# A streaming-encoder block on one core: four low parts per dense group by an adding transfer, and pair 13 by seven products

## The chip, the cores and the metric

The kernel runs on one core of one Trainium2 chip. The metric is the time on the device in microseconds (us), from the first to the last instruction of one execution of the program. Three runs of the kernel before the change took 2028.84 to 2030.45 us, with a median of 2029.99 us.

The engines have short names here: PE does matrix products (PEld is its weight load, which overlaps them), DVE is the vector engine, ACT the scalar engine, POOL is GpSimd, and SP issues most of the transfers. POOL can issue transfers too, and a transfer that POOL issues may add to what lies in its destination.

## What is computed

One layer of a hybrid encoder on x of shape (1, 256, 4096), all in float32:

```python
xn = rms_norm(x, norm_in_g)
q, k, v, z_a, a_c, g_c, z_c = split(xn @ w_in)             # w_in: 4096 x 14336
y_a = chunked_attention(q, k, v, rel_table)                # 2048 columns
y_a = rms_norm(y_a, attn_out_g) * silu(z_a)
y_c = conv_module(a_c, g_c, w_dw, ..., w_pw, b_pw)         # 2048 columns
y_c = rms_norm(y_c, conv_out_g) * silu(z_c)
h = x + concatenate([y_a, y_c]) @ w_out                    # 4096 x 4096
gate = sigmoid(rms_norm(h, ple_norm_g) @ w_ple_gate + b)   # 4096 x 4096
h = h + gate * (p @ w_ple)
out = rms_norm(h, final_g)
```

Three products with weights of 4096 rows carry nearly all of the work. The weights are read from HBM once.

## The kernel before

**Parts.** A float32 product is done as three products of shorter numbers. Each operand is split into a high part (a copy rounded to a shorter format, `fp32r`) and a low part (the number minus its high part). PE computes high x high, low activation x high weight, and high activation x low weight. The activations are split once and kept: `xT` (the input), `yT` (attention and convolution) and `hT` (the residual) are eight tiles each of four blocks, with the high and low part of 128 rows of k by 256 tokens per block. The weights are split as they stream by (`parts_of`, L199): ACT casts the tile `wt` to `wh` (L204) and DVE subtracts, `wl = wt - wh` (L205). A `wt` tile holds 128 rows of k for two column blocks of 512, 512 KB; SP issues its transfer. Five buffers hold `wt`, three each hold `wh` and `wl`.

**Products.** `mixed_product` (L344) computes two column blocks j for two halves h of the tokens, with four PSUM banks `acc`. Its k blocks are taken in 16 pairs, in an order given by a text such as `dense` (L329). A pair without a mark is plain: two tiles, 24 matmuls. A pair with "*" goes by seven products instead of eight, in the manner of Strassen: 21 matmuls. For it DVE also forms sums of weights, `ua` (L469, L470) and `ub` (L476, L477), which are split like weights into `uh` and `ul`, and four products read activation blocks that were combined beforehand (`s_of`, out of `comb` tiles). Four helper banks (`acc_P` in the profile) hold the extra products until `on_helpers` adds them up after the last seven of the group. A pair with "+" (early groups only) has its `ua` summed by a transfer of POOL that adds to what SP loaded (L423).

**Groups.** A group is one call of `mixed_product`. `dense` orders nine of them: the four groups for z of `gated` (L1064; 986 to 1314 us of the profile), the last three of w_out (1404 to 1651 us) and the last two of `gated_pair` for w_ple_gate (1743 to 1918 us). The first groups of w_out and w_ple_gate, in which their operands are still being made, use `late`, and the last group of all uses `final`. In all dense groups pairs 1, 3, 5, 7, 9, 11, 13 and 15 are plain.

At the end of a group, four evacuations read the `acc` banks: DVE adds them to the sums of the helpers (L1051 for the last product of the convolution, L1075 in `gated`, L1201 in `gated_pair`). The next group's matmuls cannot write into a bank before. This place is called a seam below. What follows the evacuations (gating, squares, adding to the residual `hc`) is put into a list, `later`, and `fill` takes some of it after each pair; in the profile these side steps have the line L184. In a w_ple_gate group there are twelve of them on DVE besides the four evacuations.

**What sets the order.** A scheduler that knows the dependencies and the tiles' buffers orders the queue of each engine when the program is built; the order of the text is where it starts from. Each engine then works strictly down its queue. An instruction that waits holds up all that stand behind it on its engine.

## Time and profile before

| what | value |
|---|---|
| runs of the kernel, median of 3 | 2029.99 us (2028.84 to 2030.45) |
| profiled execution, its span | 2027.3 us |
| matmuls on PE (`PE ... x`) | 9064 |
| ACT busy | 1222.7 us, 60% |
| `wl` by subtraction, 128x1024 | 601 times, mean 1219 ns from start to end |
| `wh` by cast, 128x1024 | 601 times, mean 1052 ns |
| transfers from HBM | 430.77 MB, 215 GB/s over the span |

The median of the runs and the span of the profiled execution are different measurements. The prediction adds up terms against the span and says how the two stand to each other.

In the timeline a row holds the start, the duration, the engine, the line, the operation, what it writes and reads, its shape and how many of the kind follow one another; in brackets stands how long the engine was idle before it and what ended that. Operations overlap a little at their ends, so that what one costs is better read from start to start. In the windows view each row is a stretch of time; behind each engine stand its busy time and the number of its instructions, then the granted clock of PE, the busy share of the transfer engines and GB/s. The groups' lines (`L205 DVE ...`) give busy time and the mean of one in ns, and behind the second bar the idle time of the engine ahead of them and what ended it.

### The profile page before, as it was taken

What the parts mean: (1) busy time and instruction counts of PE and PEld (TensorE: products, weight loads), DVE (VectorE), ACT (ScalarE), POOL (GpSimd) and SP (SyncE); (2) the same over time, 40 slices, a digit from 0 to 9 for tenths busy, and PEclk for the clock granted to TensorE, in tenths of its full rate; (3) what the DMA queues carried; (4) which work ended last, traced back from release to release, by engine and by line L of the source; (5) the groups of instructions that cost most, each with busy time, mean ns of one, the idle gap of its engine ahead of it and who ended that gap; (6) DMA issues with size and microseconds to landing.
All of it is one profiled execution on the core that took longest, in us unless ns stands there. A gap on an engine that the chain in (4) does not pass through costs nothing.

```text
span 2027.3 us, 26222 instructions
## 1 busy us (share of the span) xinstructions
PE 2010.3 (99%) x9064; PEld 1652.2 (81%) x9064; DVE 1917.8 (95%) x2732; ACT 1222.7 (60%) x1591; POOL 46.9 (2%) x50
## 2 busy tenths in 40 slices
PE   9999999999999999999999999999999999999997
PEld 7888888878888888788888888888888888888876
DVE  7999999889999998888899999999999999999998
ACT  7655545665656556776556566676665666665555
POOL 0000000000000000000000000000000000000000
PEclk9999999999999999999999999999999999999999
DMA  8787878678669867556666666676666656666765
GB/s 293 222 237 236 253 219 249 177 227 256 192 198 268 251 202 239 157 176 213 192 210 204 206 203 214 210 239 209 203 210 199 208 191 204 207 219 205 233 206 181
DMA packets 171168, 436.70 MB, mean 215 GB/s; under 512 B 13966, under 2 KB 17182, under 8 KB 171034
## 3 DMA queue, kind: packets, MB, share of 16 engines
q1 hardware_dynamic: 161952, 417.93, 64.1%
q0 software_dynamic: 8432, 16.25, 4.7%
q8 instruction: 71, 1.16, 0.3%
q10 hardware_dynamic: 650, 0.84, 0.1%
q14 instruction: 63, 0.52, 0.1%
HBM read 430.77 MB, written 4.19 MB: 215 GB/s over the span
## 4 chain that ended last, share of the span: by engine, by line
PE 92%; DVE 4%; issue 2%; DMA 1%; ACT 1%; POOLq 0%; POOL 0%; ACTq 0%; DVEq 0%
PE acc L387 71%; PE acc_P L387 17%; DVE wl L205 1%; PE tmp_ps L170 1%; DVE cv L726 1%; PE acc L229 1%; DMA wt<-in_w_in_dram 1%; DVE ul L205 1%; PE tmp_ps L898 0%; PE tmp_ps L882 0%; PE tmp_ps L916 0%; DVE cv L807 0%; PE tmp_ps L921 0%; ACT uh L204 0%; PE acc L375 0%
## 5 line engine op out<-in xcount | busy, mean ns | idle before, releaser
L387 PE MATMUL acc<-wh,big_t 128*128 128x512 f32 x4112 | 1271.6, 391 | 0.9 <-DVE y_c L1051 0.7
L204 ACT CAST wh<-wt 128x1024 fp32r<-128x1024 f32 (+1 forms) x737 | 708.8, 972 | 514.6 <-PE acc L387 359.8
L387 PEld LDWEIGHTS acc<-wh,big_t 128*128 128x128 f32 x4112 | 768.9, 188 | 160.4 <-DVE y_c L1051 1.1
L205 DVE TENSOR_TENSOR wl<-wt,wh 128x1024 fp32r<-128x1024 f32 (+1 forms) x737 | 816.7, 1120 | 33.4 <-ACT wh L204 27.8
L387 PE MATMUL acc<-wl,big_t 128*128 128x512 f32 x2056 | 794.5, 392 | 0.1
L387 PEld LDWEIGHTS acc<-wl,big_t 128*128 128x128 f32 x2056 | 385.5, 188 | 81.6 <-DVE wl L205 2.0
L204 ACT CAST uh<-ua 128x1024 fp32r<-128x1024 f32 x180 | 189.4, 1052 | 95.9 <-DVE ua L470 46.4
L205 DVE TENSOR_TENSOR ul<-ua,uh 128x1024 fp32r<-128x1024 f32 x180 | 219.5, 1220 | 5.0 <-ACT uh L204 3.2
L726 DVE SCALAR_TENSOR_TENSOR cv<-uT,dw,cv 128x255 f32<-128x255 f32 (+23 forms) x480 | 204.2, 465 | 1.1
L387 PE MATMUL acc_P<-uh,big_t 128*128 128x512 f32 x528 | 161.8, 391 | 0.1
L204 ACT CAST uh<-ub 128x1024 fp32r<-128x1024 f32 x92 | 96.8, 1052 | 92.5 <-DVE ub L477 81.1
L205 DVE TENSOR_TENSOR ul<-ub,uh 128x1024 fp32r<-128x1024 f32 x92 | 112.2, 1220 | 6.3 <-ACT uh L204 5.5
L387 PEld LDWEIGHTS acc_P<-uh,big_t 128*128 128x128 f32 x528 | 98.0, 188 | 23.0 <-ACT uh L204 3.5
L387 PE MATMUL acc_P<-ul,big_t 128*128 128x512 f32 x264 | 101.1, 391 | 0.1
L469 DVE TENSOR_TENSOR ua<-wt 128x512 f32<-128x512 f32 x105 | 72.0, 686 | 17.6 <-DMA wt<-in_w_in_dram 11.5
L387 PE MATMUL acc<-uh,big_t 128*128 128x512 f32 x272 | 84.1, 390 | 0.0
L387 PE MATMUL acc_P<-wh,big_t 128*128 128x512 f32 x272 | 84.0, 389 | 0.0
L470 DVE TENSOR_TENSOR ua<-wt 128x512 f32<-128x512 f32 x105 | 71.8, 684 | 3.2 <-DMA wt<-in_w_in_dram 3.1
L387 PE MATMUL acc_P<-uh,comb_t 128*128 128x512 f32 x228 | 70.2, 391 | 0.4 <-ACT uh L204 0.3
L477 DVE TENSOR_TENSOR ub<-ub,wt 128x512 f32<-128x512 f32 x92 | 63.1, 686 | 0.8
L476 DVE TENSOR_TENSOR ub<-ua,wt 128x512 f32<-128x512 f32 x92 | 62.9, 684 | 0.3
L387 PEld LDWEIGHTS acc<-uh,big_t 128*128 128x128 f32 x272 | 51.1, 188 | 10.6
(244 smaller groups left out, 1518.9 us busy)
## 6 DMA issues: line engine op xcount, KB each, us to landing
wt<-in_w_in_dram SPq DMA_DIRECT2D x416, 512.0 KB, 4.6
wt<-in_w_out_dram SPq DMA_DIRECT2D x128, 512.0 KB, 4.2
wt<-in_w_ple_gate_dram SPq DMA_DIRECT2D x128, 512.0 KB, 4.2
wt<-in_w_pw_dram SPq DMA_DIRECT2D x32, 512.0 KB, 4.7
ua<-in_w_in_dram SPq DMA_DIRECT2D x31, 512.0 KB, 4.5
ua<-in_w_in_dram POOLq DMA_DIRECT2D x31, 512.0 KB, 8.4
wt<-in_w_in_dram SPq DMA_DIRECT2D x31, 256.0 KB, 2.9
hc<-in_x_dram SPq DMA_DIRECT2D x8, 512.0 KB, 4.2
```

The source lines that it names most:

```text
L170: nc.tensor.transpose(pt[:, i * T + h * P : i * T + (h + 1) * P], src[:, h, b] if len(src.shape) == 4 else src[:, h, b * P : (b + 1) * P], ...
L204: nc.scalar.copy(wh[:, :kc, :], wt[:, :kc, :]),
L205: nc.vector.tensor_tensor(wl[:, :kc, :], wt[:, :kc, :], wh[:, :kc, :].bitcast(F32), ALU.subtract),
L229: nc.tensor.matmul(acc, a, b[:, k, :], start=kb == 0 and kind == 0, stop=kb == kblocks - 1 and kind == 2,)
L387: nc.tensor.matmul(banks[name], a, b, start=name not in begun, stop=final and ends[name] == n and kind == 2 and not (left and name in "P2 ...
L469: plus(ua[:, 0], w0[:, 0], w0[:, 1])
L470: plus(ua[:, 1], w0[:, 1], w1[:, 1])
L476: plus(ub[:, 0], ua[:, 0], w1[:, 1])
L477: plus(ub[:, 1], ub[:, 0], w1[:, 0])
L726: nc.vector.scalar_tensor_tensor(cv[:, i, PAD - k :], uT[:, i, : T + k - PAD], dw[:, b, k : k + 1], cv[:, i, PAD - k :], ALU.mult, ALU.add,)
```

## The change

Two things are changed in the nine dense groups, and a new order goes with them.

Four plain pairs (3, 5, 7 and 9) are marked "-". The low part of their second tile is not subtracted by DVE. Instead `high_and_minus` lets ACT make `wh` and, by a second operation, minus the same rounded numbers into a tile `low` (of the tag "stage", two buffers). Then POOL issues a transfer that reads the same weights from HBM once more and adds them onto `low`, which thereby becomes weight minus high part. The four matmuls that read `low` are put off until after the next pair (`waiting`, `add_waiting`). `compare` runs once, in the first dense group: DVE makes that tile's low part by subtraction as well, subtracts `low` from it, ACT squares and sums the difference, and the sum is added to `r_x`.

Pair 13 goes by seven products. Its combined activations have no `comb` tile; they are written into the second half of the tokens' columns of block 0 in four tiles of xT, yT and hT (`spare_places`), three times in all: after the other combinations of xT, after the first w_out group and after the first w_ple_gate group.

The tiles z of `gated` and `gated_pair` are now taken when the helper banks are summed, not at the start of the group.

```diff
+    def high_and_minus(wt):
+
+        wh = wpool.tile([P, KC, NB], F32R, tag="wh", name="wh", bufs=3)
+        nc.scalar.copy(wh, wt)
+        low = spool.tile([P, KC, NB], F32R, tag="stage", name="low")
+        nc.scalar.activation(low, wt, AF.Identity, scale=-1.0)
+        return wh, low
+
+    compared = []
+
+    def compare(wt, wh, low):
+
+        same = wpool.tile([P, KC, NB], F32R, tag="wl", name="wl", bufs=3)
+        nc.vector.tensor_tensor(same, wt, wh.bitcast(F32), ALU.subtract)
+        nc.vector.tensor_tensor(
+            same.bitcast(F32), same.bitcast(F32), low.bitcast(F32), ALU.subtract
+        )
+        apart = cpool.tile([P, KC], F32, name="apart")
+        for k in range(KC):
+            square_sum(apart[:, k : k + 1], same[:, k].bitcast(F32), scale=1e9)
+        nc.vector.tensor_tensor(r_x, r_x, apart, ALU.add)
+        compared.append(True)
...
         def split():
+            if at_places:
+                for i, (hi, lo) in enumerate(at_places):
+                    src = s[:, i * P : (i + 1) * P]
+                    nc.scalar.copy(hi, src)
+                    nc.vector.tensor_tensor(lo, src, hi.bitcast(F32), ALU.subtract)
+                return
...
-    dense = units("1 0* 3 2* 5 4* 6* 7 8* 9 10* 11 12* 14* 13 15")
+    dense = units("1 0* 2* 3- 4* 13* 5- 6* 8* 7- 10* 12* 9- 14* 11 15")
...
+    def spare_places(tiles):
+
+        return [[t[:, 0, q, P:] for q in range(2)] for t in tiles[:4]]
+
+    places = {}
+
+    def combine_into_places(pair, tiles):
+
+        rows = sum_rows()
+        places[pair] = spare_places(tiles)
+        t, i = tiles[pair // 2], pair % 2 * 2
+        combine_again(None, None, t, i, rows, at_places=places[pair])()
...
+        waiting = []
+
+        def add_waiting(n):
+
+            while waiting and waiting[0][0] <= n:
+                waiting.pop(0)[1]()
...
             if not seven:
-                for k in range(2):
-                    add_plain(n, k, *parts_of(wts[k], 2)[0])
+                add_plain(n, 0, *parts_of(wts[0], 2)[0])
+                if by_dma:
+                    wh, low = high_and_minus(wts[1])
+                    nc.gpsimd.dma_start(
+                        low, two_columns(w, 2 * pair + 1, col, apart), accum_op=ALU.add
+                    )
+                    if not compared:
+                        compare(wts[1], wh, low)
+                    add_plain(n, 1, wh, low, kinds=range(2))
+                    waiting.append((n + 1, partial(add_plain, n, 1, wh, low, kinds=(2,))))
+                else:
+                    add_plain(n, 1, *parts_of(wts[1], 2)[0])
+                add_waiting(n)
...
             def s_of(i):
+                if pair in places:
+                    return places[pair][i]
...
             add("P4", block(k1, 1), (ubh[:, 1], ubl[:, 1]), n, True)
+            add_waiting(n)
...
+    combine_into_places(13, xT)
 
     def gated(ys, c0, col, r_y, order, ahead):
 
-        _, z = sum_tiles()
+        z = []
 
         def on_helpers(helper):
+            z.extend(sum_tiles()[1])
...
+        if c0 == 0:
+            combine_into_places(13, yT)
...
     for c0 in range(0, n_f - 2, 2):
         gated_pair(c0, dense if c0 else late, None if c0 else h_ahead)
+        if c0 == 0:
+            combine_into_places(13, hT)
```

The scheduler turns this into other queues. Three places show it. A row holds the line, the operation, what it writes and reads (with the tiles' numbers), and the shape; line numbers behind the change are those of the changed kernel.

The first place is DVE's queue in the first dense group. Before, between pairs 2 and 4 of the order:

```order
L469 TENSOR_TENSOR ua_9055<-wt_9047 128x512
L205 TENSOR_TENSOR ul_8987<-ub_8983,uh_8986 128x1024
L205 TENSOR_TENSOR wl_8980<-wt_8966,wh_8979 128x1024
L470 TENSOR_TENSOR ua_9055<-wt_9047,wt_9049 128x512
L476 TENSOR_TENSOR ub_9066<-ua_9055,wt_9049 128x512
L205 TENSOR_TENSOR wl_9016<-wt_9011,wh_9015 128x1024
L205 TENSOR_TENSOR wl_9032<-wt_9013,wh_9031 128x1024
```

With the change, around the comparison (L225 and L226):

```order
L541 TENSOR_TENSOR ub_8960<-ua_8949,wt_8943 128x512
L205 TENSOR_TENSOR wl_8993<-wt_8988,wh_8992 128x1024
L542 TENSOR_TENSOR ub_8960<-ub_8960,wt_8943 128x512
L225 TENSOR_TENSOR wl_9013<-wt_8990,wh_9008 128x1024
L534 TENSOR_TENSOR ua_9038<-wt_9030 128x512
L205 TENSOR_TENSOR ul_8964<-ub_8960,uh_8963 128x1024
L226 TENSOR_TENSOR wl_9013<-wl_9013,low_9010 128x1024
L205 TENSOR_TENSOR wl_9035<-wt_9030,wh_9034 128x512
L535 TENSOR_TENSOR ua_9038<-wt_9030,wt_9032 128x512
L541 TENSOR_TENSOR ub_9049<-ua_9038,wt_9032 128x512
```

L226 reads `low`, so it stands behind the adding transfer; a `ua` and a `ul` are between it and L225, and the parts of pair 4 are behind it.

The second place is ACT's queue in the third group of `gated`, before:

```order
L204 CAST wh_10352<-wt_10348 128x512
L204 CAST uh_10359<-ua_10356 128x1024
L204 CAST wh_10363<-wt_10350 128x1024
L204 CAST uh_10370<-ub_10367 128x1024
L204 CAST wh_10399<-wt_10395 128x1024
L204 CAST wh_10415<-wt_10397 128x1024
L204 CAST wh_10435<-wt_10431 128x512
```

and with the change:

```order
L204 CAST wh_10368<-wt_10364 128x512
L204 CAST wh_10379<-wt_10366 128x1024
L217 ACTIVATE low_10433<-wt_10413 128x1024
L204 CAST wh_10415<-wt_10411 128x1024
L204 CAST uh_10375<-ua_10372 128x1024
L215 CAST wh_10431<-wt_10413 128x1024
L204 CAST uh_10386<-ub_10383 128x1024
L204 CAST wh_10448<-wt_10444 128x512
```

`low` (L217) is made ahead of the two casts of its own pair and ahead of `uh` of the seven before it.

The third place is DVE's queue near the start of the first dense group of w_ple_gate, where `hc` is the residual, before:

```order
L205 TENSOR_TENSOR wl_15636<-wt_15631,wh_15635 128x1024
L205 TENSOR_TENSOR ul_15598<-ub_15594,uh_15597 128x1024
L184 TENSOR_TENSOR hc_11657<-hc_11657,row_15401 128x512
L205 TENSOR_TENSOR wl_15652<-wt_15633,wh_15651 128x1024
L184 TENSOR_TENSOR hc_11657<-hc_11657,row_15401 128x512
L184 TENSOR_TENSOR hc_11659<-hc_11659,z_14648 128x512
L205 TENSOR_TENSOR wl_15678<-wt_15673,wh_15677 128x512
```

and with the change:

```order
L205 TENSOR_TENSOR ul_15800<-ua_15796,uh_15799 128x1024
L291 TENSOR_TENSOR comb_15670<-comb_15669 128x128
L292 SCALAR_TENSOR_TENSOR comb_15670<-comb_15669 128x128
L542 TENSOR_TENSOR ub_15807<-ub_15807,wt_15790 128x512
L293 SCALAR_TENSOR_TENSOR comb_15670<-comb_15670,comb_15669 128x128
L301 TENSOR_TENSOR big_t_14680<-comb_15670,big_t_14680 128x128
L294 SCALAR_TENSOR_TENSOR comb_15670<-comb_15669,comb_15670 128x128
L301 TENSOR_TENSOR big_t_14709<-comb_15670,big_t_14709 128x128
L184 TENSOR_TENSOR hc_11743<-hc_11743,z_15535 128x512
L301 TENSOR_TENSOR big_t_14831<-comb_15670,big_t_14831 128x128
L301 TENSOR_TENSOR big_t_14896<-comb_15670,big_t_14896 128x128
L205 TENSOR_TENSOR ul_15811<-ub_15807,uh_15810 128x1024
```

The combinations of pair 13 of hT (L291 to L301) now lie between the sums and the parts of pair 2, the second of two sevens in a row.

More of the change, by code (lines that the diff above doesn't have):

```diff
@@ L285, in combine, with combine_again @@
         combined_parts(dst, at, s, a[:, :T], pts[1][:, :P], pts[1][:, P:], g[:, 1:2])()
-    def combine_again(dst, at, t, i, rows, then=lambda ins: None):
+    def combine_again(dst, at, t, i, rows, then=lambda ins: None, at_places=None):
         a, s = rows
@@ L295, in combine_again @@
         )
-        return combined_parts(dst, at, s, a[:, :T], a[:, T : T + P], a[:, T + P :], 1.0, then)
+        return combined_parts(
+            dst, at, s, a[:, :T], a[:, T : T + P], a[:, T + P :], 1.0, then, at_places
+        )
     def comb_tile(combs, n_kept=0):
@@ L324, in units @@
     def units(text):
-        return [(int(u.rstrip("*+")), u[-1] if u[-1] in "*+" else "") for u in text.split()]
-    dense = units("1 0* 3 2* 5 4* 6* 7 8* 9 10* 11 12* 14* 13 15")
+        return [
+            (int(u.rstrip("*+-")), "".join(f for f in "*+" if f in u), "-" in u)
+            for u in text.split()
+        ]
+    dense = units("1 0* 2* 3- 4* 13* 5- 6* 8* 7- 10* 12* 9- 14* 11 15")
     first = units("0 1 3 5 7 9 11 13 15 2* 8 4* 10 6* 12 14")
@@ L358, in mixed_product @@
         n_left = len(left) // 2
-        for n, (_, seven) in enumerate(order[: len(order) - n_left]):
+        for n, (_, seven, _) in enumerate(order[: len(order) - n_left]):
             for name in ("P1", "P5", "P6", "P7", "P2", "P3", "P4") if seven else ("P2", "P3", "P4", "X"):
@@ L429, in mixed_product @@
                 after.enter_context(tc.issue_after(ins.ins))
-        last_seven = max((n for n, (_, seven) in enumerate(order) if seven), default=None)
-        for n, (pair, seven) in enumerate(order):
+        last_seven = max((n for n, (_, seven, _) in enumerate(order) if seven), default=None)
+        for n, (pair, seven, by_dma) in enumerate(order):
             if n < done:
@@ L1171, in gated_pair @@
     def gated_pair(c0, order, ahead):
-        _, z = sum_tiles()
-        rows, fgs = [], []
+        z, rows, fgs = [], [], []
         def on_begin():
@@ L1179, in on_helpers @@
         def on_helpers(helper):
+            z.extend(sum_tiles()[1])
             stt(z[0][0], helper["P1"], r_h[:, :1], rows[0], ALU.mult, ALU.add)
```

3 lines of the change are left out of this document (2 added, 1 removed).

## The prediction

> **What bounds the kernel now.** I began with the page's busy times and chain of waits, then its queues.
>
> ```profile
> span 2027.3 us, 26222 instructions
> PE 2010.3 (99%) x9064; PEld 1652.2 (81%) x9064; DVE 1917.8 (95%) x2732; ACT 1222.7 (60%) x1591; POOL 46.9 (2%) x50
> ...
> q0 software_dynamic: 8432, 16.25, 4.7%
> ...
> PE 92%; DVE 4%; issue 2%; DMA 1%; ACT 1%; POOLq 0%; POOL 0%; ACTq 0%; DVEq 0%
> ```
>
> PE is the bound, with 92% of the chain, but DVE is busy for 95% of the span and holds most of what is left. So the question is not whether fewer matmuls help, but where DVE is late. The windows view gives that by stage: one gated group, one w_out group and the two w_ple_gate groups.
>
> ```profile
> core 0: us, PE busy (x) PEld busy (x) DVE busy (x) ACT busy (x) POOL busy (x), PEclk, DMA share, GB/s
> 1149.70:1231.00 81.30, 81.28 (x359) 67.00 (x358) 78.15 (x93) 49.02 (x54) 0.00 (x0) 1.00 0.65 207
> 1485.60:1567.60 82.00, 81.89 (x362) 67.48 (x361) 78.16 (x93) 48.84 (x58) 0.00 (x0) 1.00 0.63 205
> 1742.90:1829.00 86.10, 86.05 (x378) 70.16 (x377) 85.53 (x105) 53.38 (x64) 0.00 (x0) 1.00 0.66 211
> 1829.00:1918.30 89.30, 89.30 (x392) 72.75 (x391) 88.37 (x107) 52.50 (x64) 0.00 (x0) 1.00 0.68 216
> ```
>
> PE runs without gaps: 81.30/359 = 0.2265 us from one matmul to the next, at a granted clock of 1.00. DVE is at 78.15/81.30 = 96% in the gated and 95% in the w_out group, and at 99% in both w_ple_gate groups. In these two it has no slack at all.
>
> **Unit costs.** The timeline of DVE gives start-to-start times:
>
> ```profile
> 1184.53 1.22 DVE L205 TENSOR_TENSOR wl<-wt,wh 128x1024 fp32r<-128x1024 f32 x1
> 1185.66 0.68 DVE L470 TENSOR_TENSOR ua<-wt 128x512 f32<-128x512 f32 x1
> 1186.27 0.68 DVE L205 TENSOR_TENSOR wl<-wt,wh 128x512 fp32r<-128x512 f32 x1
> 1186.87 0.68 DVE L476 TENSOR_TENSOR ub<-ua,wt 128x512 f32<-128x512 f32 x1
> ```
>
> 1.135 us for a 128x1024 operation, 0.60 for a 128x512 one. So a plain pair costs DVE 2 x 1.135 = 2.27 and PE 24 x 0.2265 = 5.44. A pair by seven products costs DVE three 1024s and five 512s, 6.4, and PE 21 matmuls, 4.76. A pair with the new "-" costs DVE 1.135. A plain unit therefore gains DVE 3.2 us on PE, a seven loses 1.65, a "-" gains 4.3. How far DVE is ahead at a place, its lead, decides whether PE stands.
>
> **The change part by part, for nine dense groups.**
>
> *Matmuls.* Pair 13 goes from 24 to 21 in each: 27 x 0.2265 = **-6.1 us**. This is certain if PE is kept fed.
>
> *DVE per group.* Pair 13: 6.4 - 2.27 = +4.1. Four low parts: -4 x 1.135 = -4.5. Net -0.4, while PE loses 0.7. DVE's share rises slightly; the change shifts DVE's burden to the front of the group (0* 2* 4* 13* among the first six units) and lightens its end.
>
> *The low parts.* ACT gets a second 1024 operation on each such block (a cast there takes 1.05 us), 36 in all; at 49 busy of 81 it has room. The transfer is then issued by POOL. The same kind of transfer exists in the early groups:
>
> ```profile
> L204 ACT CAST wh<-wt 128x1024 fp32r<-128x1024 f32 x601 | 624.5, 1052 | 426.4 <-PE acc L387 304.8 <-issue 25.8 <-DVE cv L726 17.8
> L423 POOL DMA_DIRECT2D ua<-in_w_in_dram x31: 1213/1222/1359, 89.9 to 787.2; - x31
> DMA to landing us min/median/max: 6.1/8.4/10.4
> ```
>
> It lands 8.4 us after its issue, at worst 10.4. The four matmuls that read `low` wait until after the next unit. A cast now ends some 3.3 us ahead of its first matmul:
>
> ```profile
> 1000.02 1.05 ACT L204 CAST wh<-wt 128x1024 fp32r<-128x1024 f32 x1
> 1004.38 0.62 PE L387 MATMUL acc<-wh,big_t 128*128 128x512 f32 x2
> ```
>
> To these 3.3 come the 20 other matmuls of the pair (4.5) and the next unit (4.8, a seven): 12.6 us against 8.4. It is hidden, with 4.2 to spare and 2.2 at worst: 0. Without that cover each place would cost what the landing exceeds 12.6 by. The new rows on POOL stand behind no other work there in these stages (busy 0.00 in the windows), and at some 15 us between issues not behind one another.
>
> *Traffic.* 4.7% of 2027 us over 31 transfers is 3.07 us of all 16 engines for each, so four per group raise the DMA share from 0.65 by 4 x 3.07/81 = 0.15, to 0.80. What that does to the weights' loads:
>
> ```profile
> wt<-in_w_in_dram SPq DMA_DIRECT2D x416, 512.0 KB, 4.6
> wt<-in_w_out_dram SPq DMA_DIRECT2D x128, 512.0 KB, 4.2
> L469 DVE TENSOR_TENSOR ua<-wt 128x512 f32<-128x512 f32 x105 | 72.0, 686 | 17.6 <-DMA wt<-in_w_in_dram 11.5 <-DMA wt<-in_w_out_dram 4.3 <-DMA wt<-in_w_ple_gate_dram 1.2
> ```
>
> A load lands 0.4 later in w_in, where adding transfers run, than in w_out, where none do. From 0 to 36 x 0.4 = 14; DVE waits for weights before the first `ua` for only 17.6 us in the whole run, with a lead behind it, so I take the low end, **+0.5**.
>
> *The comparison, once.* In the first dense group DVE makes two more 1024s (2.3 us, beside an addition on two columns), and the second 1024 waits for the transfer. On ACT `low` is made ahead of two casts, so the first subtraction comes at least 2 x 0.95 after it, and between it and the second stand a `ua` and a `ul`: 1.9 + 1.135 + 0.6 + 1.135 = 4.8 us. DVE, in queue order, is up to 1.3 later. So DVE waits 8.4 less 4.8 to 6.1: 2.3 to 3.6, say 3.0 (bounds 0, from 6.1 to land, and 5.6, from 10.4). Behind the waiting instruction stand the next seven's `wl`, `ua`, `ub`, and PE waits for these. The lead there today:
>
> ```profile
> 1001.68 1.22 DVE L205 TENSOR_TENSOR wl<-wt,wh 128x1024 fp32r<-128x1024 f32 x1
> 1004.83 0.39 PE L387 MATMUL acc<-wl,big_t 128*128 128x512 f32 x1
> ```
>
> 1004.83 - 1002.90 = 1.9 us. So PE stands 3.0 + 2.3 - 1.9 = **+3.4** (0 to 6). Nothing later gives this back, since PE has no other idle time to fill there.
>
> The Trainium skill, "DMA: Bandwidth & Descriptors", section "Anatomy of one DMA - SWDGE (gpsimd) path", gives a fixed 2.0 us plus the bytes at 436 GB/s for such a transfer, so an estimate of 3.2 us for 512 KB. By it the wait would vanish and the sum be 3.0 lower. This trace, with 6.1 at the least, disagrees for adding transfers, and I keep 8.4.
>
> *The seams of the gated groups.* The planner now puts a `wl` behind the first of four evacuations at three seams and, in exchange, moves one away from the first seam. What that does is seen there:
>
> ```profile
> 984.78 0.68 DVE L1051 TENSOR_TENSOR y_c<-acc,row 128x512 f32<-128x512 f32 x1
> 985.38 1.21 DVE L205 TENSOR_TENSOR wl<-wt,wh 128x1024 fp32r<-128x1024 f32 x1
> 986.51 1.88 DVE L1051 TENSOR_TENSOR y_c<-acc,row 128x512 f32<-128x512 f32 x3
> ...
> 986.20 0.39 PE L387 MATMUL acc<-wl,big_t 128*128 128x512 f32 x1
> 987.25 0.73 PE L387 MATMUL acc<-wh,big_t 128*128 128x512 f32 x2 [0.67 <-DVE y_c L1051]
> ...
> 1068.07 0.39 PE L387 MATMUL acc<-wl,big_t 128*128 128x512 f32 x1
> 1068.68 0.70 PE L387 MATMUL acc<-wh,big_t 128*128 128x512 f32 x2 [0.22 <-DVE z L1075]
> ```
>
> 987.25 comes 1.05 after 986.20 instead of 0.23: 0.82 lost. A seam with all four together, at 1068.68, loses 0.61 - 0.23 = 0.38; of the two others that are so today one lies after it at half that and one at nothing. So 3 x 0.82 - 0.82 - 0.57 = **+1.1** (0 to 2.5).
>
> *The w_ple_gate groups.* Here leads are gone. The count of DVE's work against PE's from the group's start, evacuations (4, 2.64 us) and twelve side steps (L184, 0.60 each, 7.2) included:
>
> ```profile
> 1742.86 2.72 DVE L1201 SCALAR_TENSOR_TENSOR z<-acc,r_h,z 128x512 f32<-128x512 f32 x4
> 1745.50 1.22 DVE L205 TENSOR_TENSOR wl<-wt,wh 128x1024 fp32r<-128x1024 f32 x1
> ...
> 1784.13 0.61 PE L387 MATMUL acc_P<-wh,big_t 128*128 128x512 f32 x2
> 1784.80 0.74 PE L387 MATMUL acc_P<-uh,big_t 128*128 128x512 f32 x2
> ```
>
> Before, the worst place is after 1 0* 3 2* 5 4* 6*: DVE 2.64 + 7.2 + 3 x 2.27 + 4 x 6.4 = 42.3, PE 3 x 5.44 + 4 x 4.76 = 35.4; DVE needs 6.9 more. PE stands for little there (1784.80 is 0.2 late; with its neighbours 0.4), so the lead at the start is about 6.5. Now it is after 1 0* 2* 3- 4* 13*: DVE 2.64 + 7.2 + 2.27 + 1.135 + 25.6 = 38.9, PE 10.9 + 19.0 = 29.9; 9.0 more. PE stands 2.5 instead of 0.4: +2.1 in the second group. In the first, the combinations of pair 13 fall into the same stretch. Their kind is seen at
>
> ```profile
> 969.13 0.69 DVE L291 TENSOR_TENSOR comb<-big_t 128x512 f32<-128x512 f32 x1
> 969.73 0.28 DVE L271 SCALAR_TENSOR_TENSOR comb<-comb 128x128 f32<-128x128 f32 x1
> 970.05 0.29 DVE L268 TENSOR_TENSOR comb<-comb 128x128 f32<-128x128 f32 x1
> 970.26 0.28 DVE L269 SCALAR_TENSOR_TENSOR comb<-comb 128x128 f32<-128x128 f32 x1
> 970.46 1.22 DVE L205 TENSOR_TENSOR wl<-wt,wh 128x1024 fp32r<-128x1024 f32 x1
> ```
>
> eight small ones of 0.2 inside the stretch, 1.6 more: 2.1 + 1.6 = 3.7. Together **+5.8** (0, if side steps and lead absorb all, to 7). The other two sets of combinations (2.2 us each) fall where DVE has 4%: 0.
>
> *The w_out groups.* Two sevens in a row cost the lead 2 x 1.65 after one plain pair's +3.2, where now the two kinds alternate. The waits of PE's weight loads in all three groups today are one row:
>
> ```profile
> PEld acc_P L387 <- DVE ul L205: 0.5, 1, 0.5
> ```
>
> I estimate as much in each group in its place, 3 x 0.5 - 0.5 = **+1.0** (0, if the two plain pairs that end the group before leave a lead, to 4, if each second seven costs its 1.65 less that 0.5).
>
> Sum: -6.1 + 0.5 + 3.4 + 1.1 + 5.8 + 1.0 = +5.7 on the span of 2027.3, so 2033.0. The median of the runs, 2029.99, stands 2.7 above that span, so **2035.7 us**.
>
> **The rivals.**
>
> *B, the stalls are absorbed.* DVE has 0.4 us less per group and the front's burden is met by the lead of the group before. For it: 4% slack in seven groups. Against it: 99% in two. Then -6.1, traffic 0.5 and about a microsecond for the comparison: 2025.4, faster. It holds if the lead at the start of a w_ple_gate group is above 9.
>
> *C, the transfer is quick.* At 6.1 us to land, the least of the 31 rows, the comparison waits for nothing: 2035.7 - 3.0 = 2032.7; with one w_ple_gate peak absorbed too, 2030.6. Both are the same as before within 0.2%. Against it: a median of 8.4.
>
> *D, the low parts arrive late.* If, at a DMA share of 0.80 instead of 0.65, a landing takes over 12.6 us, PE stands at each of 36 places. At 13 us that is 0.4 x 36 = 14 on top: 2050, slower. For it: POOL's next transfer has only been seen with the one before it landed, and 10.4 is not far from 12.6. Against: a spread of 6.1 to 10.4 at the highest shares of the run. The Trainium skill, "SBUF - State Buffer", section "SBUF: two separate sides", warns that DVE can keep GpSimd from writing a transfer's descriptors; here all 31 issues took 1213 to 1359 ns beside a DVE 95% busy, so no such lock is seen.
>
> That the change does not do what it says is no rival: the new order has 27 matmuls fewer and 36 more transfers on POOL.
>
> **How the numbers follow.** Forecast A 0.47 (its own range 2031.5 to 2040), B 0.20, C 0.15, D 0.18. About 0.2%, 4.06 us, is what a measurement of this kernel can tell from no change, so "same" is 2025.9 to 2034.05. Faster: nearly all of B, and a little of C, 0.20. Same: C, a rest of B, and A's low quarter, 0.27. Slower: A's rest and D, 0.53. The range runs from B's time to the middle of D, 2025.5 to 2047: it leaves out about half of B and half of D.
>
> **What would show it.** Right: PE stands some 3 us in the first dense group behind the second operation of the comparison, which waits for the transfer; PE waits for `ul` or `uh` at 2* and 13* of both w_ple_gate groups, some 6 us together; 0.8 at three seams with a `wl` between evacuations; no wait of PE for `low`. Wrong: matmuls that wait for `low` (D), loads of weights that land well above 4.6, or a w_ple_gate group no longer per matmul than 0.2265 (B).

## The result and the profile after

The changed kernel took 2051.7 us (median of 4 runs, 2050.91 to 2053.21) against 2029.41 us before, a ratio of 1.0108 with a 95% interval of 1.0094 to 1.0123: 22 us slower, where 6 were forecast, and above the range. Lines of its page that answer to those shown of before:

```profile
span 2050.3 us, 26398 instructions
PE 2022.9 (99%) x9037; PEld 1647.1 (80%) x9037; DVE 1924.1 (94%) x2780; ACT 1270.1 (62%) x1661; POOL 78.3 (4%) x86
...
q0 software_dynamic: 13616, 35.13, 10.1%
...
PE 85%; DVE 8%; issue 3%; DMA 2%; ACT 1%; ACTq 0%; POOLq 0%; POOL 0%; DVEq 0%; SPq 0%
```

PE has 27 matmuls fewer, as forecast, yet is busy 12.6 us longer, and its share of the chain of waits fell from 92% to 85% in favour of DVE, issues and transfers. Matmuls became slower, and waits were added. The windows view of the same four groups as before (third gated group, second dense w_out group, both w_ple_gate groups):

```profile
1149.60:1234.10 84.50, 84.08 (x365) 67.66 (x364) 78.16 (x96) 54.34 (x61) 3.46 (x4) 1.00 0.74 224
1491.70:1577.10 85.40, 83.50 (x360) 66.89 (x359) 77.65 (x96) 53.20 (x63) 3.48 (x4) 1.00 0.71 222
1755.20:1848.00 92.80, 89.52 (x376) 70.86 (x375) 87.45 (x116) 59.72 (x74) 3.52 (x4) 0.98 0.73 224
1848.00:1940.20 92.20, 89.55 (x382) 70.79 (x381) 87.41 (x108) 57.88 (x70) 3.46 (x4) 1.00 0.74 228
```

They are 3.2, 3.4, 6.7 and 2.9 us longer. DVE, with 78.16 of 84.50 us, is no longer at 96%: it waits too. The view of waits from 984 to 1945 us names for whom (us in all, times, longest):

```profile
ACT low L217 <- DMA wt<-in_w_out_dram: 12.0, 7, 3.0
PEld acc_P L434 <- ACT uh L204: 11.6, 20, 2.1
DVE ua L535 <- DMA wt<-in_w_out_dram: 8.9, 5, 3.2
ACT low L217 <- DMA wt<-in_w_in_dram: 7.0, 11, 1.2
PE acc_P L434 <- ACT uh L204: 5.1, 6, 1.7
PE acc L434 <- DVE wl L205: 3.1, 3, 1.7
ACT low L217 <- DMA wt<-in_w_ple_gate_dram: 2.6, 2, 1.4
```

The same window of before has no row of PE waiting for `uh` or `wl`, and these:

```profile
DVE ua L469 <- DMA wt<-in_w_in_dram: 7.8, 8, 1.7
PEld acc_P L387 <- ACT uh L204: 2.2, 9, 0.5
DVE ua L470 <- DMA wt<-in_w_in_dram: 1.6, 3, 0.9
```

With the change ACT waits 21.6 us at the instruction that makes `low`, for weights that have not landed, and DVE waits for weights at the sums `ua`, mostly at the one that needs the pair's second tile (L535). PE then waits for `uh` and `wl`, which stand behind these two. One such place, in the timeline of the changed kernel in the first w_ple_gate group, first a row of DVE, then two of ACT and one of PE:

```profile
1802.45 0.69 DVE L542 TENSOR_TENSOR ub<-ub,wt 128x512 f32<-128x512 f32 x1
...
1804.92 1.06 ACT L217 ACTIVATE low<-wt 128x1024 fp32r<-128x1024 f32 x1 [1.15 <-DMA wt<-in_w_ple_gate_dram]
1805.88 1.03 ACT L204 CAST uh<-ub 128x1024 fp32r<-128x1024 f32 x1
...
1806.96 0.73 PE L434 MATMUL acc_P<-uh,big_t 128*128 128x512 f32 x2 [1.34 <-ACT uh L204]
```

The sum for that `uh` was ready at 1803.1, but its cast had to wait until 1805.88 behind `low`, and PE with it. Last, the groups' lines of the second gated group (1070 to 1150 us) before:

```profile
L387 PE MATMUL acc<-wl,big_t 128*128 128x512 f32 x76 | 29.6, 389 | 0.0
L387 PE MATMUL acc_P<-uh,big_t 128*128 128x512 f32 x36 | 11.1, 389 | 0.0
```

and after:

```profile
L434 PE MATMUL acc<-wl,big_t 128*128 128x512 f32 x53 | 20.5, 389 | 0.0
L434 PE MATMUL acc_P<-uh,big_t 128*128 128x512 f32 x42 | 13.2, 396 | 0.0
L434 PE MATMUL acc<-low,big_t 128*128 128x512 f32 x16 | 4.4, 396 | 0.0
```

A matmul that reads `uh`, `ul` or `low` takes 7 ns longer, one that reads `wl` does not, and nothing waits. From start to start the mean over the group, which I call its pace, is 0.2303 us instead of 0.2267. Nothing in the forecast gives this.

### The profile page after: what moved, and what is told of

Same layout as the page of the kernel before. It is cut to its first block, busy times and chain, and to the rows that moved or that the text cites. A ratio compares the mean times of both kernels' runs of the same rounds, so it can differ in the third digit from the quotient of the medians.

```text
span 2050.3 us, 26398 instructions
## 1 busy us (share of the span) xinstructions
PE 2022.9 (99%) x9037; PEld 1647.1 (80%) x9037; DVE 1924.1 (94%) x2780; ACT 1270.1 (62%) x1661; POOL 78.3 (4%) x86
## 3 DMA queue, kind: packets, MB, share of 16 engines
q0 software_dynamic: 13616, 35.13, 10.1%
## 4 chain that ended last, share of the span: by engine, by line
PE 85%; DVE 8%; issue 3%; DMA 2%; ACT 1%; ACTq 0%; POOLq 0%; POOL 0%; DVEq 0%; SPq 0%
PE acc L434 65%; PE acc_P L434 16%; DVE wl L205 3%; DVE ul L205 1%; DMA wt<-in_w_in_dram 1%; PE tmp_ps L170 1%; DVE cv L794 1%; PE acc L252 1%; ACT uh L204 1%; DMA wt<-in_w_ple_gate_dram 1%; ACT wh L204 0%; DVE ua L535 0%; DVE ua L534 0%; DVE ub L541 0%; DMA wt<-in_w_out_dram 0%
## 5 line engine op out<-in xcount | busy, mean ns | idle before, releaser
L434 PE MATMUL acc<-wh,big_t 128*128 128x512 f32 x4004 | 1226.7, 392 | 1.2 <-DVE z L1145 1.1
L204 ACT CAST wh<-wt 128x1024 fp32r<-128x1024 f32 (+1 forms) x701 | 666.8, 961 | 456.0 <-PE acc L434 349.8
L434 PEld LDWEIGHTS acc<-wh,big_t 128*128 128x128 f32 x4004 | 749.4, 188 | 160.1 <-DVE z L1145 2.2
L205 DVE TENSOR_TENSOR wl<-wt,wh 128x1024 fp32r<-128x1024 f32 (+1 forms) x701 | 773.8, 1113 | 42.9 <-ACT wh L204 37.3
L434 PE MATMUL acc<-wl,big_t 128*128 128x512 f32 x1858 | 718.6, 393 | 3.3 <-DVE wl L205 3.1
L434 PEld LDWEIGHTS acc<-wl,big_t 128*128 128x128 f32 x1858 | 348.9, 188 | 79.6 <-DVE wl L205 6.8
L205 DVE TENSOR_TENSOR ul<-ua,uh 128x1024 fp32r<-128x1024 f32 x189 | 231.2, 1223 | 9.2 <-ACT uh L204 6.0
L434 PE MATMUL acc_P<-uh,big_t 128*128 128x512 f32 x582 | 181.2, 397 | 4.9 <-ACT uh L204 4.9
L535 DVE TENSOR_TENSOR ua<-wt 128x512 f32<-128x512 f32 x114 | 78.3, 687 | 17.3 <-DMA wt<-in_w_out_dram 8.9
L534 DVE TENSOR_TENSOR ua<-wt 128x512 f32<-128x512 f32 x114 | 78.2, 686 | 8.1 <-DMA wt<-in_w_in_dram 6.6
L434 PEld LDWEIGHTS acc_P<-ul,big_t 128*128 128x128 f32 x291 | 54.6, 188 | 17.5 <-DVE ul L205 4.7
```

Source lines behind the costliest of these rows:

```text
L204: nc.scalar.copy(wh[:, :kc, :], wt[:, :kc, :]),
L205: nc.vector.tensor_tensor(wl[:, :kc, :], wt[:, :kc, :], wh[:, :kc, :].bitcast(F32), ALU.subtract),
L434: nc.tensor.matmul(banks[name], a, b, start=name not in begun, stop=final and ends[name] == n and kind == 2 and not (left and name in "P2 ...
L534: plus(ua[:, 0], w0[:, 0], w0[:, 1])
L535: plus(ua[:, 1], w0[:, 1], w1[:, 1])
```

## The experiments

Eighteen kernels ran, in five sets with the kernel before beside each; its medians are 2029.4, 2029.8, 2028.8, 2029.3 and 2029.6 us, and each ratio is against that of its own set. Of the changed kernels all but the second one here (64 bytes) leave the comparison out. I speak of a stall where the start of a matmul is over 0.3 us behind the one before it; its size is that distance less 0.2265.

**Is it where the tiles lie?** The new tile `apart` holds 8 bytes per partition, takes 32 in the built program, and everything allocated behind it on its side (`wh`, `wl`, xT, yT, hT) moves by 32 bytes; `uh`, `ul` and `low` lie on the other side and stay.

```diff
 kernel before, one tile at the end of the small ones made wider
-    end = cpool.tile([P, 2, NH], F32, name="end")
+    end = cpool.tile([P, 6, NH], F32, name="end")[:, :2]
```

> The kernel before with one small tile made 32 bytes wider, so that every tile of one side of the on-chip memory (weights' wh and wl, activations xT, yT, hT) lies 32 bytes further, as in the changed kernel, while uh, ul and z stay; no instruction is added or moved. Theory A (the matmuls of the changed kernel go at 0.230 instead of 0.2267 us in the dense groups because of where the tiles lie): matmuls that read uh and ul at 0.233 to 0.234 from about 986 us on, the rest of the loss beside them, and a time 9 to 13 us above before, 2039 to 2043. Theory B (the adding transfers of POOL, or the second read of the weights, slow the matmuls): no change, 2029 to 2031.

2037.0 us, ratio 1.0043 (1.0030 to 1.0055): 7.7 us for 32 bytes, with the queues of all engines the same, row by row. In the same group:

```profile
L387 PE MATMUL acc<-wl,big_t 128*128 128x512 f32 x75 | 29.2, 389 | 0.0
L387 PE MATMUL acc_P<-uh,big_t 128*128 128x512 f32 x36 | 11.3, 396 | 0.0
```

The loss is under theory A's 9 to 13, but the slower matmuls are the ones that it names. The same widening of the changed kernel, 64 bytes in all:

> The changed kernel with one small tile made 32 bytes wider, so that the same tiles lie 64 instead of 32 bytes further than before; queues word for word those of the changed kernel. Theory A, in the form that 64 bytes is the step that counts: matmuls back at 0.2267, 8 to 12 us gained, 2040 to 2044; a little less than the pace alone because DVE, which is late at the stalls, gets no faster. Theory A in the form that only the old place is good: as the changed kernel, 2051. Theory B: as the changed kernel, 2051 to 2052.

2054.9 us; `uh` at 395 ns. So 64 bytes are not a step that heals it.

> The changed kernel without the one comparison of a low part made by transfer with one made by subtraction (compare is not called, nothing is added to r_x); its small tile goes with it, so that all tiles lie as before. Theory A: the tile, not the comparison's work, is what costs: within 2 us of the run with 64 bytes, 2038 to 2044, and the first dense group at most 1 us shorter than there. Rival (the comparison's wait for the transfer costs the 3.4 us that I predicted, and the tiles' place nothing): 2048.

```diff
-                    if not compared:
-                        compare(wts[1], wh, low)
```

2052.7 us (2051.59 to 2057.91): no gain, against theory A's 2038 to 2044 and its rival's 2048. The tiles lay as before again, and the pace was 0.2276. But other waits took the place of the slow matmuls: the third gated group came down from 84.5 to 82.0 us, the first w_ple_gate group from 92.8 to 91.4, while the first dense w_out group rose from 82.2 to 85.3, with a granted clock of 0.98:

```profile
1409.50:1494.80 85.30, 83.03 (x355) 66.71 (x354) 80.16 (x99) 54.78 (x64) 3.48 (x4) 0.98 0.72 224
```

So the 7.7 us do not add to the rest: with the faster pace the stalls of the nine dense groups in its profile grew from 21.5 to some 30 us. The place of the tiles costs where PE is the bound; where PE waits for others, a faster PE waits longer.

One more run tells what about the place counts. It adds to the first kernel here a tile of 224 bytes ahead of `uh`, `ul` and z:

```diff
+    pool("pad", 1, side=1).tile([P, 56], F32, name="pad")
     spool = upool = pool("lpool", 2, side=1)
```

> The kernel before with all tiles moved: those of one side by 32 bytes as in the first run, and uh, ul and z by 224 bytes, so that all weights and activations again lie at the same remainder to 256 bytes, but at 0 instead of 224. If what counts is that the operands of a matmul lie alike: pace back at 0.2268, 2029 to 2031 (a few of the queues' rows stand otherwise, up to 2 us). If the remainder itself counts: 0.2296 or slower, and 2037 or more.

2029.05 us, ratio 0.9997 (0.9988 to 1.0007), `uh` at 389 ns. All operands then lie at remainder 0 to 256 bytes, before at 224; both are fast. So what counts is that the two sides lie alike. That 256 bytes are the period is not shown; the runs have the pairs 224 and 224, 0 and 0, 224 and 0, and 224 and 32.

**ACT's queue.**

```diff
-        nc.scalar.activation(low, wt, AF.Identity, scale=-1.0)
+        with queued_behind(before):
+            nc.scalar.activation(low, wt, AF.Identity, scale=-1.0)
```

Here `before` holds the cast `uh` of the pair before, and `queued_behind` gives the scheduler this order.

> As the run without the comparison, and ACT makes low only behind the cast uh of the pair before (an order added to the scheduler; nothing else is changed in the text). Theory C (low stands at the head of ACT's queue and waits there for its weights, 21.6 us in 20 places of the changed kernel, and holds up uh and wh behind it, for which PE then waits): 4 to 9 us faster than the run without the comparison, and ACT's waits ahead of low fall below 8 us. Rival D (the stalls come from DVE alone, which has two pairs by seven products one behind the other): within 2 us of the run without the comparison.

2045.0 us, 7.7 less than without this edit: theory C, by its numbers, and ACT waits for nothing ahead of `low` any more. The three w_out groups have stalls of 3.6 us together instead of 12.6. The two w_ple_gate groups got worse, at 93.7 and 95.5 us, since there `low` is now late itself:

```profile
PEld acc L435 <- DMA low<-in_w_ple_gate_dram: 10.3, 6, 3.3
PE acc L435 <- DMA low<-in_w_ple_gate_dram: 8.0, 4, 2.9
```

That is rival D of the prediction, brought about by the mending of another wait.

**The w_ple_gate groups.**

```diff
-        gated_pair(c0, dense if c0 else late, None if c0 else h_ahead)
-        if c0 == 0:
-            combine_into_places(13, hT)
+        gated_pair(c0, dense_old if c0 else late, None if c0 else h_ahead)
```

`dense_old` is the order of before.

> As the run with low behind uh, but the two w_ple_gate groups take the order of before (no low part by transfer, pair 13 plain, no combinations of hT); the gated and w_out groups keep the change. Theory E (in the w_ple_gate groups, where DVE was 99% busy, the front of the new order cannot be paid at all, and low's place does not matter there): their stalls fall from 17.2 us to about 1, their six matmuls come back (+1.4), so 2045.0 - 16 + 1.4: 2029 to 2032, no faster than before. Rival F (the two groups suffer from something that starts earlier, late weights or the put-off matmuls): 2036 or more.

2032.1 us, ratio 1.0010 (1.0001 to 1.0018), at the upper edge of theory E. Of the nearly 16 us over before that the run ahead of it had, 13 went with the change in these two groups.

**One half of the change alone.** Low parts by transfer in the old order:

```diff
-    dense = units("1 0* 2* 3- 4* 13* 5- 6* 8* 7- 10* 12* 9- 14* 11 15")
+    dense = units("1 0* 3- 2* 5- 4* 6* 7- 8* 9- 10* 11 12* 14* 13 15")
```

> Low parts by transfer alone: the order of before with pairs 3, 5, 7 and 9 marked; pair 13 plain, no combinations in spare blocks, no comparison, tiles where they lay before. DVE is spared 36 operations of 1.135 us. Theory G (the transfers, and ACT's queue with low at the head, cost time by themselves): PE stalls in the groups of w_out and gated stay at 1 to 4 us each, 2036 to 2045, slower than before although DVE has less to do. Rival H (pair 13 by seven products and its order are the cost; sparing DVE is harmless): 2028 to 2031.

2083.0 us, ratio 1.0256: far beyond theory G's 2045, although DVE has 41 us less to do than before, by the unit cost. And pair 13 by seven products without any transfer, in the new order (its marks "-" taken out):

> Pair 13 by seven products in the new order, but all low parts by subtraction on DVE (no transfers on POOL, no low on ACT), no comparison, tiles where they lay before. DVE has 4.1 us more per group, against 78 of 81 busy before. Theory D/E (DVE late): DVE is the bound of all nine groups, each some 2 to 3 us longer than before and the w_ple_gate groups 5 to 8 longer, 2050 to 2065. Theory G (ACT's queue and the transfers are the cost, DVE is not): 2026 to 2036, faster than the run without the comparison by over 15.

2046.7 us: neither theory's number. DVE is short, but by less than I took: 80.85 of 82.80 us in the third gated group, and 92.51 of 92.80 in the first w_ple_gate group, which is 6.7 us longer than before:

```profile
1149.00:1231.80 82.80, 82.66 (x358) 65.66 (x357) 80.85 (x98) 49.31 (x56) 0.00 (x0) 1.00 0.66 204
1750.40:1843.20 92.80, 89.60 (x384) 70.26 (x383) 92.51 (x121) 56.40 (x71) 0.00 (x0) 1.00 0.64 199
```

**What the transfers cost.** First the 2083 us again, with `low` behind `uh` and behind the first `wh` of its pair:

> The run with low parts by transfer alone (order of before, pair 13 plain), with low made on ACT behind the pair before's uh and its own pair's first wh. Theory C (ACT's queue): from 2083 down to 2031 to 2045. Rival J (transfers collide with the loads of weights, whatever ACT does): 2065 or more.

2094.4 us, worse: so putting `low` back does not help here, against theory C, and rival J's bound of 2065 is passed. Then with every low part subtracted by DVE and `low` read by nobody:

```diff
-                    add_plain(n, 1, wh, low, kinds=range(2))
-                    waiting.append((n + 1, partial(add_plain, n, 1, wh, low, kinds=(2,))))
-                else:
-                    add_plain(n, 1, *parts_of(wts[1], 2)[0])
+                add_plain(n, 1, *parts_of(wts[1], 2)[0])
```

> The kernel before with the 36 low parts made on ACT and by transfer as in the run ahead of this, but read by nobody: all matmuls take low parts subtracted by DVE. DVE's and PE's work is that of before; added are 36 us on ACT and the traffic. Theory C: 2029 to 2034, both are harmless where nothing waits behind them. Rival J: 2045 or more.

2072.1 us: 43 us for 36 transfers that nobody waits for. Three kernels differ only in the transfer, with the same queues on PE, DVE, ACT and SP:

```diff
-                        low, two_columns(w, 2 * pair + 1, col, apart), accum_op=ALU.add
+                        low[:, :, :16], two_columns(w, 2 * pair + 1, col, apart)[:, :, :16],
+                        accum_op=ALU.add,
```

> The run with unread low parts, whose 36 adding transfers take 16 columns instead of 512 each (1/32 of the bytes); the queues of all engines are the same otherwise. Nobody reads low. Theory J (the traffic of the adding transfers delays the loads of weights, and DVE waits with a sum at the head of its queue): 2029 to 2036, the 43 us go with the bytes. Rival K (the order that the scheduler made and ACT's 36 us cost the 43): 2068 to 2074.

```diff
-                    nc.gpsimd.dma_start(
-                        low, two_columns(w, 2 * pair + 1, col, apart), accum_op=ALU.add
-                    )
+                    nc.gpsimd.dma_start(low, two_columns(w, 2 * pair + 1, col, apart).bitcast(F32R))
```

> The same with full transfers that copy instead of adding (low then holds the weights; nobody reads it). Theory J in the form that the adding itself is dear (3.07 us of all 16 engines each, where a plain 512 KB takes 1.6): about half of the 43 us goes, 2045 to 2058. Theory J by bytes alone: as with adding, 2068 to 2074.

With 1/32 of the bytes 2037.0 us, with a full copy 2048.7, with a full addition 2072.1. So of the 43 us some 8 stay with the small transfers (ACT's work, the order of the queues and the transfers themselves, which these runs do not part), 12 go with the bytes and 23 with the adding. The four runs with copies lie between 2043.5 and 2055.0, so that the 12 and the 23 are known to some 5 us. The view of waits, from 984 to 1960 us, has PE's waits for `wl` (us in all, times, longest). With the small transfers:

```profile
PE acc L433 <- DVE wl L205: 1.2, 3, 0.8
```

with the copies

```profile
PE acc L433 <- DVE wl L205: 4.4, 7, 1.2
```

and with the additions

```profile
PE acc L433 <- DVE wl L205: 22.1, 19, 3.3
```

How it comes about stands in the timeline of the last of them:

```profile
1091.47 0.86 POOL L510 DMA_DIRECT2D low<-in_w_in_dram  x1 [9.42 <-ACT low L216]
...
1099.60 0.69 DVE L531 TENSOR_TENSOR ua<-wt 128x512 f32<-128x512 f32 x1 [2.10 <-DMA wt<-in_w_in_dram]
1100.21 1.22 DVE L205 TENSOR_TENSOR ul<-ub,uh 128x1024 fp32r<-128x1024 f32 x1
1101.34 1.22 DVE L205 TENSOR_TENSOR wl<-wt,wh 128x1024 fp32r<-128x1024 f32 x1
...
1102.62 0.50 PE L433 MATMUL acc<-wl,big_t 128*128 128x512 f32 x1 [0.72 <-DVE wl L205]
```

The weights that `ua` waits for were issued at 1092.18, 0.7 us behind POOL's transfer, and landed at 1099.58, after 7.4 us. DVE stands at that sum, the `wl` that PE needs is behind it, and the next load cannot be issued before DVE has freed a buffer. Sorted over the stages from 985 to 1960 us of that trace, 106 loads that overlap an adding transfer by more than 1.5 us land after a median of 5.7 us, the others after 4.3. With the copies the same sorting gives 4.7 and 4.4.

**Another order.** The first marked pair comes ahead of the second seven, and each later one a place earlier against the sevens:

```diff
-    dense = units("1 0* 2* 3- 4* 13* 5- 6* 8* 7- 10* 12* 9- 14* 11 15")
+    dense = units("1 0* 3- 2* 4* 5- 6* 13* 7- 8* 10* 9- 12* 14* 11 15")
```

> As the run with low behind uh, with another order in all nine groups: 1 0* 3- 2* 4* 5- 6* 13* 7- 8* 10* 9- 12* 14* 11 15, in which a marked pair comes ahead of the second seven and never three sevens stand around one. Theory E (the front of the order costs DVE its lead): the w_ple_gate stalls fall from 17.2 to 4 to 10 us, the others stay near 1 each; 2031 to 2039. Rival I (in those groups any seven more is too much for DVE, whatever the order): as the run with low behind uh, 2043 to 2047.

2038.1 us, 6.9 less than with the order of the change, within theory E. The four gated groups have stalls of 0.6 us in all instead of 3.4; the w_ple_gate groups still have 12.7 (theory E had 4 to 10).

> The same order in the gated and w_out groups only; the w_ple_gate groups as in the kernel before. Theory E: stalls of the seven groups fall from 1.1 to below 0.5 each, and what is left of six groups' 0.68 us shows: 2026 to 2029, at or below the kernel before. Rival J (the transfers hold the weights up wherever they stand): 2031 to 2034, no better than the run with the order of the change there.

2028.4 us, ratio 0.9997 (0.9985 to 1.0010): theory E's number, but the eleven runs spread from 2024.2 to 2038.8. The same order with neither transfers nor marks:

> The spread order in the gated and w_out groups, w_ple_gate as before, and no transfer at all: pair 13 by seven products, every low part subtracted by DVE. Theory D (DVE has 82.3 us of work for 80.6 us of matmuls in such a group): each of the six or seven groups 1 to 2 us longer than with the transfers, 2033 to 2040. If the transfers are not needed for it: 2024 to 2029.

2038.3 us, theory D. For pair 13 the transfers are worth 8 to 10 us in seven groups (against 2030.5 and 2028.4 with them), while in the old order, with pair 13 plain, nine groups of them cost 54. That they pay where DVE is short of time, and cost where it is not, is the reading that fits both; no run varies DVE's work alone.

> The best run so far (the spread order in the gated and w_out groups, w_ple_gate as before) with three transfers a group instead of four: pair 9 is subtracted by DVE again. DVE then has about 79 of 80.6 us per group. Theory J: less traffic, fewer late weights, less spread between runs and 0 to 2 us gained, 2025 to 2028. Theory D (DVE is short): 1 to 3 us lost, 2029 to 2032.

```diff
-    dense = units("1 0* 3- 2* 4* 5- 6* 13* 7- 8* 10* 9- 12* 14* 11 15")
+    dense = units("1 0* 3- 2* 4* 5- 6* 13* 7- 8* 10* 9 12* 14* 11 15")
```

**2025.3 us** (ten runs, 2024.73 to 2026.97), ratio 0.9979 (0.9970 to 0.9989): the only version whose whole interval lies below the kernel before. The third gated group and the second dense w_out group run without a gap, with DVE at 98% and 97%:

```profile
1148.00:1229.20 81.20, 81.20 (x360) 67.23 (x359) 79.19 (x97) 53.53 (x59) 2.61 (x3) 1.00 0.76 227
1483.10:1564.20 81.10, 81.10 (x360) 67.12 (x359) 78.60 (x96) 53.31 (x64) 2.60 (x3) 1.00 0.75 227
```

The last two ran beside it.

> The spread order with its four transfers in the four gated groups only; w_out and w_ple_gate as in the kernel before. By the profiles the gated groups took 325.8 us in the best run so far against 329.3 before, and the w_out groups 245.7 against 246.8: 2025 to 2027, and less spread, as 16 transfers instead of 28 are left.

2032.4 us (2027.90 to 2042.07), a miss. In its profile two gated groups, with the very order and marks of the version with four transfers, have stalls of 6.1 and 3.4 us where that one's first profile had 0.5 and 0.1. In each of the two, DVE waits over 3 us for weights at a sum `ua`, and PE then waits 3 us for `wl`.

> The best run so far once more beside the two others, as its eleven runs spread from 2024.2 to 2038.8: 2026 to 2030.

2030.5 us (2025.80 to 2033.96), in a profile with stalls of 2.5 and 2.9 us in the second and third gated groups, where the first profile of the same kernel had 0.5 and none. So these stalls differ from run to run of one kernel. Four transfers a group spread over 8 us here and over almost 15 the first time, three over 2.

## Why the prediction was wrong, step by step

The forecast was 16 us too low. Two of its steps failed in their mechanism: that the low parts are hidden because ACT has room, and that the traffic can be put at the low end because DVE's lead covers it. The other costs were mis-sized, two of them too high, and one cost was in no term. Over the nine dense groups the changed kernel is 21.4 us longer. By the starts of its matmuls that is 6.1 us less for the matmuls saved, stalls of 21.5 us instead of 3.0, and some 9 us for slower matmuls. How the added stalls divide between ACT's queue, late loads and DVE's own work stays open, since what the runs take away does not add up.

- **Matmuls, -6.1.** Right, and hidden. It shows where nothing else is in the way: the best version has seven groups changed, 7 x 3 x 0.2265 = 4.8 us, and is 4.3 us faster than before.
- **The low parts, hidden, 0.** The forecast looked at when `low` is read, and there it held: in the changed kernel PE never waits for it. It failed in "ACT has room". The order quoted above showed `low` ahead of the casts of its own pair and of `uh`; I took ACT's 49 of 81 busy for slack and did not ask whether its weights are there. Moving `low` back took 7.7 us away.
- **Traffic, +0.5 (0 to 14).** This is the step that failed most by its mechanism, though only the kernel in the old order shows a price by itself: 35 of 43 us go with the bytes and the adding. I took the difference of two medians, 4.6 against 4.2, and covered it by DVE's lead. The loads of the four gated groups before have landings (least, median, most) of

```profile
DMA to landing us min/median/max: 3.4/4.1/6.9
```

  and with the change, from 986 to 1320 us,

```profile
DMA to landing us min/median/max: 3.3/4.9/9.1
```

  In the changed kernel the 127 loads of the stages from 985 to 1940 us that overlap an adding transfer land after a median of 5.9 us, the others after 4.3. The early groups before, from 100 to 780 us, where POOL's adding transfers run, have

```profile
DMA to landing us min/median/max: 3.5/4.8/9.4
```

  So the tail was in the trace of before: sorted as above, loads there land after 5.2 us beside an adding transfer (one in ten after 8.1) and after 3.9 otherwise. The median of all loads for w_in, 4.6, mixes the two kinds. A ring of five buffers, in which eight of the sums already waited for their weights before (the row of 7.8 us above), had little lead against a load that is 3 us late.
- **The comparison, +3.4 (0 to 6).** Wrong. `low`, issued at 996.4, was there within 5.8 us instead of 8.4, and DVE stood at the second subtraction for less than 0.2 us:

```profile
1000.88 1.21 DVE L205 TENSOR_TENSOR ul<-ub,uh 128x1024 fp32r<-128x1024 f32 x1
1002.18 1.23 DVE L226 TENSOR_TENSOR wl<-wl,low 128x1024 f32<-128x1024 f32 x1
```

  The first dense group became 0.6 us shorter. The median of 31 adding transfers in another stage was no measure; the 36 new ones land after 7.4 (5.4 to 9.9). By the estimate of 3.2 us from the Trainium skill's "DMA: Bandwidth & Descriptors", section "Anatomy of one DMA - SWDGE (gpsimd) path", the wait vanishes too, but no adding transfer here came near that figure; the quickest of the 36 took 5.4.
- **The seams, +1.1.** Too high: the `wl` stands between the evacuations as forecast, and PE waits for z 1.1 us where it waited 0.9 for y_c and z.
- **The w_ple_gate groups, +5.8.** The place was right, the size half: they are 6.7 and 2.9 us longer with 1.4 us of matmuls less, so 11, and PE waits there for `uh` and `ul` as forecast. I counted DVE's work alone; `uh` also stood behind ACT's `low` and late weights, as in the rows above, and no lead is left. How much of the 11 is DVE's own work is not shown. Undoing these two groups gave 13 us in one version and 9.7 in another.
- **The w_out groups, +1.0.** Mis-sized by far: 1.0, 3.4 and 2.7 us longer with 2.0 of matmuls less, so 9. Some 3.5 of it are the slower matmuls and 5.6 are stalls. The stalls come from ACT's `low` and late weights more than from the two sevens in a row: with `low` moved back, in the same order, 3.6 of 12.6 us of stalls were left.
- **The place of the tiles** was in no term: 7.7 us alone, though taking it back in the changed kernel gained nothing.

Of the signs named ahead, that of loads which land well above 4.6 us came; PE's wait behind the comparison did not, and neither, in the changed kernel, did matmuls that wait for `low`.

## What to carry to other kernels

A transfer's price is not its own landing but what it does to the loads beside it: look at the tail of the landings where such transfers already run, and ask which queue stands still when one load is 3 us late. An engine that is 60% busy can still be the bound through one instruction at the head of its queue that waits. And a few bytes of a new small tile can move every large one: compare how long the same instruction takes on the same tiles, before looking for a cause in the work that was added.

## What the runs showed of the hardware

A matmul here reads a tile made from weights, 128x512, and a block of activations, 128x128. Where the first lay at another remainder to 256 bytes than the second (224 against 0 or 32), the matmul took 395 or 396 ns instead of 389, and some 0.234 us from start to start instead of 0.2265; these are three to four in ten of a gated group's matmuls. With both at 224, or both at 0, all were fast. Which two accesses meet there is open.

An adding transfer of 512 KB delays its neighbours more than a copy of the same bytes: 23 us more in 36 transfers; the share of the transfer engines' time for POOL's queue is 7.8% with the copies and 10.1% with the additions.

A wait of PE can be paid twice. In the run with changed gated groups alone PE stood for 2.9 of 4 us, and the granted clock was then 0.50 for 5.5 us:

```profile
1128.00:1132.00 4.00, 1.07 (x5) 0.61 (x4) 3.93 (x5) 1.33 (x2) 0.00 (x0) 0.85 0.03 10
1132.00:1137.50 5.50, 5.50 (x14) 4.24 (x15) 4.17 (x5) 2.09 (x2) 0.00 (x0) 0.50 0.85 282
```

14 matmuls took the time of 24. The Trainium skill, "TensorE: Matmul & The Clock Gate", section "Part 1: The HAM clock gate", has half the clock after an idle window of about 3.4 us; here it came after a wait of 2.9 us, and in the changed kernel after two of 0.9 and 0.7 us within 3 us, behind which the clock from 1780 to 1783 us was 0.50 as well. The length of the wait does not settle it: in the same run a wait of 3.1 us that ended at 1299.7 left the clock at 1.00, and so did one of 3.3 us that ended at 1217.6 in the run with unread low parts.

What these traces do show is a grid. Within each trace that has several, the times at which the granted clock falls to 0.50 lie whole multiples of 3.413 us apart. I cut the traces of before, of the changed kernel and of the eighteen others along this grid from 980 to 1960 us. In the 15 stretches that end with such a fall PE was idle for 0.58 to 0.95 of the stretch, and in no other at full clock for more than 0.61 (by the starts of the matmuls). The wait of 2.9 us lay with 0.64 in one stretch; that of 3.1 us was shared by two, with 0.47 and 0.51.
